# One-hot bias rows as tiles, other units behind a half-way copy, and value blocks read out after the next split: one change to a hybrid decoder layer on one core

## The chip, the core and the metric

The kernel runs on one core of a Trainium2 chip. A core has several engines that run side by side and wait for each other by semaphores: TensorE (PE in the profile; PEld is its loading of stationary operands), VectorE (DVE), ScalarE (ACT), GpSimd (POOL) and SyncE (SP, which issues most of the DMA loads). Matrix products are accumulated in PSUM and read out from there by DVE or ACT.

The metric is the device time of one execution in microseconds (us). Three runs of the kernel before took 1171.28, 1173.89 and 1175.08 us; their median, 1173.89 us, is the time before. A further execution was taken with the profiler.

## What is computed

One layer of a decoder on 256 tokens with 2048 channels, in float32. The input is normalised and multiplied by one wide matrix, the result is cut into the inputs of four mixers, and a sigmoid gate with a bias of its own weighs each mixer's output before one last product:

```python
h = rms_norm(x, g_pre[l])
proj = h @ w_in[l]
...
y_a = pool_mixer(a_val, a_gate, w_pool[l], pool_scale[l])
y_b = swa_mixer(sq, sk, sv, s_gate)
y_c = gla_mixer(cq, ck, cv, c_lr, c_gate, w_alpha[l], b_alpha[l], g_gla[l])
y_m = mem_attn(mq, m_gate, mem, g_mem[l], w_mem_kv[l])
gates = jax.nn.sigmoid(g_logits.reshape(B, S, N_BRANCH, D_MODEL) + b_merge[l])
merged = (gates[:, :, 0] * (y_a @ w_br_pool[l]) + gates[:, :, 1] * (y_b @ w_br_swa[l])
          + gates[:, :, 2] * (y_c @ w_br_gla[l]) + gates[:, :, 3] * (y_m @ w_br_mem[l]))
x = x + rms_norm(merged @ w_out[l], g_post[l])
```

The change touches the gates (`g_logits` and `b_merge`, 8192 columns of `w_in`) and the two value products `cv` (gated linear attention) and `sv` (sliding-window attention).

## The kernel before

**Products in three parts.** Every weight is loaded as float32 and split: ACT writes the rounded part `hi`, DVE the rest `lo = raw - hi` (`split_w`, L149 to L154; five buffers for each of the two). A product is then three matmuls, hi by hi, lo by hi and hi by lo (`mm3`, L156 to L160). The loads land in `raw` tiles (`load_raw`, L144, issued by SP), and a split of 1024 columns serves six or more matmuls.

**Units.** The main line of work is a list of units in program order. `b_unit` (L197) makes 128 output channels for all tokens from two half units of 16 matmuls each, eight with 512 moving columns (L208) and eight with 256 (L209); `a_block` (L162) makes up to 512 output channels for two halves of the tokens, in two PSUM buffers of the tag `acc`, which has two buffers in all. The order is: the units cq and ck, three `cv` blocks, cg, the units of the memory attention (mq, mg), those of the pooling mixer (av, ag), three `sv` blocks, those of the sliding window (sq, sk, sg). After that come the products of the four branches and the last product.

**Reading out a block.** `a_block` returns a function `finish` that reads its two accumulators out (for `cv` and `sv` two ACT copies, L550 and L831). With the argument `late`, a block calls the function of the block before it right behind its own first split (`behind()` orders those instructions after the two of the split); before the change only the blocks of the last product use that, while the `cv` and `sv` blocks call `finish` at once.

**Gates as a second stream.** The gates are computed between the units. `gates(work)` (L109) is called after each half unit and each part of a block: it adds 1.13 times the work to a credit and then takes steps from a generator while the credit is above zero; each step yields what is taken off. A half unit counts 2.8. There are eight pairs of gate blocks, `gate_pair(b, jj)` (L463), whose name in the profile is made of b and jj. A pair has three stretches:

- eight small steps `gu` (loop over u and hf, L472 to L481): one split and six matmuls each into the PSUM buffer `p1`, which starts with the bias matmul. After the fourth step ACT copies `p1` to the tile `p1c` (L480), and the next four steps go on adding into `p1`. PE may not write `p1` before that copy is done. The steps are named gu{pair}{u}{hf}: gu..11 is the fourth, gu..20 the fifth.
- eight big steps `gt` (L487 to L501): one load, three additions on DVE, two splits and twelve matmuls into four PSUM buffers q4 to q7; q5 starts with the pair's second bias matmul.
- four small steps `gv` into q5 (L510 to L518), and the gate values (tanh on ACT, L459) go out to DRAM (L461, issued by ACT).

**Bias rows.** `brow` holds the biases as 16 rows of 512 in two parts (48 rows with the gap between them), `sel` has one column for each gate block or pair with ones where its rows are. The bias matmul (L454) takes one column of `sel`, repeated 128 times by its access pattern, as the stationary operand.

**Buffers.** Temporaries of up to 2 KB per partition share the tag `c2` with seven buffers (L54): among them `p1c`, the gate values on their way out, and the temporaries of the units' read-outs.

**What sets the order.** Each engine runs its instructions in a fixed order, worked out when the kernel is built: instructions that are ready go in program order, and one further down may go first where those ahead of it aren't ready. So the order on an engine is near the program's order but not the same; for instance the bias matmul of q5 runs before the steps of `p1` in the first pair (84.36 us in the trace, the first step of p1 later).

Of the kernel before, what the change touches and what calls it, by code (L numbers as in the profile page):

```python
# [8 lines left out]
F32 = mybir.dt.float32  # L9
R = mybir.dt.float32r  # L10
# [4 lines left out]
P = 128  # L15
# [22 lines left out]
def kernel(ctx, tc, ins, out):  # L38
    nc = tc.nc
    ten, vec, act, pool, sync = nc.tensor, nc.vector, nc.scalar, nc.gpsimd, nc.sync  # L40
# [13 lines left out]
    def c2(name, shape, dt=F32):  # L54
        return big.tile(shape, dt, tag="c2", bufs=NB_C2, name=name)
# [106 lines left out]
    def a_block(name, units, stat, nw, evac, load=None, per_split=None, other=False, late=None):  # L162

        accs = [seven(f"{name}a{t}") if other else acc(f"{name}a{t}", [P, 512]) for t in range(2)]
        nk = 4 * len(units)
        for u, src in enumerate(units):
            raw = load_raw(src, 4 * nw) if load is None else load(u, src)
            nk_s = max(1, 1024 // nw) if per_split is None else per_split(u)
            for hf in range(4 // nk_s):
                hi, lo = split_w(raw[:, hf * nk_s * nw : (hf + 1) * nk_s * nw], nk_s * nw, f"{name}{u}{hf}")  # L170
                if late is not None:
                    with behind():
                        late()
                    late = None
                for t in range(2):
                    ts = slice(t * P, (t + 1) * P)
                    for kk in range(nk_s):
                        k = 4 * u + nk_s * hf + kk
                        ws = slice(kk * nw, (kk + 1) * nw)
                        sh, sl = stat(k)  # L180
                        mm3(accs[t][:, :nw], sh[:, ts], sl[:, ts], hi[:, ws], lo[:, ws], k == 0, k == nk - 1)
                if hf % 2 == 0:
                    pull(1)
                gates(nk_s * 6 * (nw / 2.4 + 14) * 1e-3)
            pull(1)

        def finish():
            for t in range(2):
                evac(t, accs[t][:, :nw])

        return finish
# [5 lines left out]
    def b_unit(name, src, mov, evac, ready=None):  # L197

        a = acc(f"{name}a", [P, 512])
        if ready is None:  # L200
            raw = load_raw(src, 2048)
        for hf in range(2):
            hi, lo = ready[hf] if ready else split_w(raw[:, hf * 1024 : (hf + 1) * 1024], 1024, f"{name}{hf}")
            for kk in range(8):
                k = 8 * hf + kk
                ws = slice(kk * P, (kk + 1) * P)
                mh, _ = mov(k)
                ten.matmul(a[:], lhsT=hi[:, ws], rhs=mov.both(k), start=(k == 0), stop=False)  # L208
                ten.matmul(a[:, :T], lhsT=lo[:, ws], rhs=mh, start=False, stop=(k == KT - 1))  # L209
            if hf == 0:  # L210
                pull(1)
                gates(2.8)
        if pinned[0]:
            with behind():
                evac(name, a)
        else:
            evac(name, a)
        pull(1)
        gates(2.8)
# [90 lines left out]
    h_at = hilo_tiles("x")  # L310
# [117 lines left out]
    brow = cst.tile([48, 512], R, name="brow")  # L428
    sel = cst.tile([48, 24], R, name="sel")
# [21 lines left out]
        yield  # L451

    def bias(o, r):
        ten.matmul(o, lhsT=sel[:, r : r + 1].to_broadcast([48, P]), rhs=brow[:], start=True, stop=False)  # L454

    gate_dram = {}

# [5 lines left out]
    def gate_pair(b, jj):  # L463


        j0, j1, n = 2 * jj, 2 * jj + 1, f"{b}{jj}"
        w = ins["w_g"]
        p1 = seven(f"p1{n}")
        bias(p1[:], 4 * b + j0)
        p1c = c2(f"p1c{n}", [P, 512])  # L470
        for u in range(4):
            raw = load_raw(w[b, j0, u], 2048)  # L472
            for hf in range(2):
                hi, lo = split_w(raw[:, hf * 1024 : (hf + 1) * 1024], 1024, f"gu{n}{u}{hf}")
                for i in range(2):
                    k = 4 * u + 2 * hf + i
                    ws = slice(i * 512, (i + 1) * 512)
                    mm3(p1[:], *tok(0, k), hi[:, ws], lo[:, ws], False, k % 8 == 7, k >= 8)
                if u == 1 and hf == 1:
                    act.activation(p1c[:], p1[:], AF.Copy)  # L480
                yield 0.8  # L481
        c11 = c2(f"c11{n}", [P, 512])
        put_gate(b, j0, 0, p1[:], c11[:])
        q4, q5, q6, q7 = [seven(f"q{i}{n}") for i in (4, 5, 6, 7)]
        bias(q5[:], 16 + 2 * b + jj)
        for kk in range(8):
            raw = new_raw()  # L487
            r4 = raw[:].rearrange("p (j u c) -> p j u c", j=2, u=2)
            u, cs = kk // 4, slice((kk % 4) * 512, (kk % 4 + 1) * 512)
            sync.dma_start(r4, w[b, j0 : j0 + 2, u : u + 3 : 2, :, cs].rearrange("j u p c -> p j u c"))  # L490
            vec.tensor_tensor(r4[:, :, 0, :], r4[:, :, 0, :], r4[:, 1, :, :], op=ALU.add)  # L491
            vec.tensor_tensor(r4[:, 1, 1, :], r4[:, 1, 1, :], r4[:, 0, 0, :], op=ALU.add)  # L492
            hi, lo = split_w(raw[:, 1024:2048], 1024, f"gt{n}{kk}a")
            st, sp = kk == 0, kk == 7
            mm3(q7[:], *quart(2, kk), hi[:, 0:512], lo[:, 0:512], st, sp)
            mm3(q6[:], *quart(1, kk), hi[:, 512:1024], lo[:, 512:1024], st, sp)
            vec.tensor_tensor(r4[:, 0, 1, :], r4[:, 0, 1, :], r4[:, 1, 1, :], op=ALU.add)  # L497
            hi, lo = split_w(raw[:, 0:1024], 1024, f"gt{n}{kk}b")
            mm3(q5[:], *quart(0, kk), hi[:, 0:512], lo[:, 0:512], False, sp)
            mm3(q4[:], *tok(1, kk + 8), hi[:, 512:1024], lo[:, 512:1024], st, sp)  # L500
            yield 6.6  # L501
        v3, c21 = c2(f"v3{n}", [P, 512]), c2(f"c21{n}", [P, 512])
        vec.tensor_tensor(p1c[:], q6[:], p1c[:], op=ALU.subtract)
        vec.tensor_tensor(v3[:], q7[:], p1c[:], op=ALU.add)
        vec.tensor_tensor(c21[:], q4[:], v3[:], op=ALU.subtract)  # L505
        put_gate(b, j0, 1, c21[:], c21[:])
        vec.tensor_tensor(v3[:], q5[:], v3[:], op=ALU.add)
        put_gate(b, j1, 1, v3[:], v3[:])
        vec.tensor_tensor(q5[:], q5[:], p1c[:], op=ALU.add)
        for u in range(2, 4):  # L510
            raw = load_raw(w[b, j1, u], 2048)
            for hf in range(2):
                hi, lo = split_w(raw[:, hf * 1024 : (hf + 1) * 1024], 1024, f"gv{n}{u}{hf}")
                for i in range(2):
                    kk = 4 * (u - 2) + 2 * hf + i
                    ws = slice(i * 512, (i + 1) * 512)
                    mm3(q5[:], *quart(3, kk), hi[:, ws], lo[:, ws], False, kk == 7, True)
                yield 0.8  # L518
        c12 = c2(f"c12{n}", [P, 512])
        put_gate(b, j1, 0, q5[:], c12[:])  # L520
# [20 lines left out]
    cv = e8("cv", [P, 2, 1024])  # L541
# [4 lines left out]
    def cv_evac(j):  # L546
        def evac(t, a):
            c0, n = CV_BLOCKS[j]
            nv = min(n, 1024 - c0)
            act.activation(cv[:, t, c0 : c0 + nv], a[:, :nv], AF.Copy)  # L550
            if nv < n:
                act.activation(lr[:, t, :], a[:, nv:n], AF.Copy)

        return evac
# [136 lines left out]
    for n in range(8):  # L691
        if n == 6:
            drain("quarters")
            pinned[0] = False
            gate_stream[0] = all_gates()
        if n < 6:
            ahead[cqk[n + 1][0]] = b_split(*cqk[n + 1])
        evac = plain_evac(gq[:, n, :], SCALE) if n < 4 else plain_evac(gk[:, n - 4, :])
        b_unit(*cqk[n], h_at, evac, ahead.pop(cqk[n][0], None))
    for j in range(3):  # L700
        c0, n = CV_BLOCKS[j]
        a_block(f"cv{j}", [ins[f"w_cv{j}"][u] for u in range(4)], h_at, n, cv_evac(j))()
    queue.append(("mnorm", m_norm()))
    queue.append(("gla", gla()))
    for h in range(4):
# [109 lines left out]
    for g in (3, 2, 1, 0):  # L815
        u = c4(f"u{g}", [P, 2, PAD + T])
# [10 lines left out]
    sv = [c4(f"sv{g}", [P, 2, 512]) for g in range(3)]  # L827

    def sv_evac(j):
        def evac(t, a):  # L830
            act.activation(sv[j][:, t, :], a, AF.Copy)  # L831

        return evac

    for j in range(3):
        a_block(f"sv{j}", [ins["w_sv"][j, u] for u in range(4)], h_at, 512, sv_evac(j))()
    yb_dram = [spill("ybd", [P, 2, 4, T], R)]
    sgate = c4("sgate", [P, 4, T])

# [141 lines left out]
    late = None  # L981
# [114 lines left out]
```

## Time and profile before

| | us |
|---|---|
| median of three runs | 1173.89 |
| least and most of them | 1171.28, 1175.08 |
| the profiled execution | 1172.68 |
| its span, first to last instruction | 1170.6 |

In the profile, a row of the timeline gives the start from the beginning of the span, the length (both in us), the engine, the line of the kernel, the operation, what it writes and reads, the shapes, and in brackets how long the engine stood idle before it and what ended the wait. A row `PE p L158 <- ACT p1c L480: 2.4, 4, 0.9` in the view of waits says that PE waited with a matmul of line 158 into p for the instruction of line 480 on ACT: 2.4 us in all, four times, 0.9 the longest. The granted TensorE clock of the core is 0.998 over the span. A matmul's length covers its whole way through the array, and the next one starts well before it ends; so the distance from start to start is what a matmul costs.

### The profile page before, as it was taken

To read this page: it belongs to the slowest core of one execution; us is meant where nothing else is said; L and a number is where in the kernel's file an instruction comes from. 1 tells how busy PE (TensorE), PEld (TensorE's weight loads), DVE (VectorE), ACT (ScalarE), POOL (GpSimd) and SP (SyncE) were. 2 spreads that over 40 slices of the span, in tenths; PEclk is the share of its full clock that TensorE was granted. 3 is DMA by queue.
4 is the path that set the end of the run, shared out by engine and by line. 5 is a ranking of instruction groups with operands and counts; after the bars stand their busy time and mean duration, and the time that the engine had idled before them with its cause. 6 is when DMAs were issued, how large, how long until landed. Compare 5 with 4: busy or idle time off the path is not lost.

```text
span 1170.6 us, 15411 instructions
## 1 busy us (share of the span) xinstructions
PE 1149.8 (98%) x5854; PEld 968.2 (83%) x5854; DVE 961.2 (82%) x1201; ACT 647.0 (55%) x823; POOL 59.0 (5%) x109
## 2 busy tenths in 40 slices
PE   9999999999999999999999999999999999999997
PEld 7887898878888888878888887888788888888887
DVE  7979798999898799889989988987898676777454
ACT  7656456665655555665566556566555543434441
POOL 0010000000101001000000000000000102110000
PEclk9999999999999999999999999999999999999999
DMA  9755679757868688777788777876778988759321
GB/s 356 316 182 193 217 251 343 277 203 281 304 238 284 217 297 289 259 251 263 276 295 315 251 263 271 294 253 231 272 252 303 372 308 306 252 206 381 118 73 73
DMA packets 79946, 303.94 MB, mean 260 GB/s; under 512 B 6224, under 2 KB 8656, under 8 KB 57344
## 3 DMA queue, kind: packets, MB, share of 16 engines
q1 hardware_dynamic: 65568, 268.45, 63.5%
q0 software_dynamic: 8976, 24.91, 6.1%
q10 hardware_dynamic: 5328, 9.60, 2.2%
q8 instruction: 46, 0.75, 0.3%
q14 instruction: 28, 0.23, 0.1%
HBM read 285.11 MB, written 17.83 MB: 259 GB/s over the span
## 4 chain that ended last, share of the span: by engine, by line
PE 76%; DVE 5%; DMA 3%; ACT 2%; issue 2%; DVEq 0%; POOLq 0%; POOL 0%; ACTq 0%
PE q L158 5%; PE q L159 5%; PE q L160 5%; DMA raw<-in_w_g 2%; PE p L158 2%; PE p L159 1%; PE p L160 1%; PE sv2a L159 1%; PE sv0a L158 1%; PE sv0a L160 1%; PE o0a L160 1%; PE sv2a L158 1%; PE o0a L158 1%; PE sv1a L158 1%; PE sv0a L159 1%
## 5 line engine op out<-in xcount | busy, mean ns | idle before, releaser
L491 DVE TENSOR_TENSOR raw<-raw 128x1024 f32<-128x1024 f32 x64 | 78.1, 1220 | 8.9 <-DMA raw<-in_w_g 8.9
L497 DVE TENSOR_TENSOR raw<-raw 128x512 f32<-128x512 f32 x64 | 44.5, 696 | 1.1
L492 DVE TENSOR_TENSOR raw<-raw 128x512 f32<-128x512 f32 x64 | 44.5, 697 | 0.5
L918 POOL DMA_DIRECT2D g<-gd x32 | 17.4, 554 | 98.6 <-DVE merged L926 66.7
L926 DVE TENSOR_TENSOR merged<-merged,g 128x512 f32<-128x512 f32 x24 | 15.5, 686 | 0.0
L710 POOL DMA_DIRECT2D cgd<-cgate x4 | 2.2, 552 | 201.7 <-DVE cgate L241 201.7
L885 POOL DMA_DIRECT2D ybd<-ybt x4 | 2.7, 678 | 174.1 <-DVE ybt L247 174.1
L853 PE MATMUL sp<-k,q 128*128 128x128 f32 (+1 forms) x48 | 10.2, 335 | 1.0 <-DVE k L226 1.0
L861 ACT ACTIVATE s<-s,st 128x384 f32<-128x384 f32 (+1 forms) x8 | 6.2, 769 | 6.7 <-DVE st L860 6.7
L853 PEld LDWEIGHTS sp<-k,q 128*128 128x128 f32 x48 | 7.4, 190 | 2.9 <-DVE k L226 1.4
L856 DVE SCALAR_TENSOR_TENSOR s<-big_cst,sp 128x128 f32<-128x128 f32 (+1 forms) x24 | 7.1, 349 | 2.0 <-PE sp L853 2.0
L246 ACT ACTIVATE xhl<-xn 128x1024 fp32r<-128x1024 f32 x4 | 4.2, 1060 | 7.0 <-DVE xn L330 7.0
L459 ACT ACTIVATE c<-c 128x512 f32<-128x512 f32 x8 | 5.0, 628 | 5.5 <-DVE c L505 3.9
L939 ACT ACTIVATE mTh<-mtp 128x512 fp32r<-128x512 f32 x8 | 4.3, 595 | 6.3 <-PE mtp L937 6.3
L459 ACT ACTIVATE c<-p 128x512 f32<-128x512 f32 x8 | 4.7, 587 | 5.1 <-PE p L160 5.1
L664 POOL TENSOR_TENSOR ms<-ms,half 128x2 f32<-128x2 f32 x4 | 5.7, 1428 | 35.2 <-DVE ms L663 35.2
L879 PE MATMUL po<-pt,sv 128*128 128x256 f32 x24 | 7.2, 384 | 0.2 <-ACT pt L874 0.2
L812 POOL DMA_DIRECT2D yad<-yat x4 | 2.7, 686 | 88.5 <-DVE yat L247 88.5
L360 DVE SCALAR_TENSOR_TENSOR mhl<-mr,vecs,mhl 128x256 fp32r<-128x256 f32 x16 | 6.8, 479 | 0.4 <-issue 0.3
L652 POOL TENSOR_TENSOR sq<-sq 128x256 f32<-128x256 f32 x4 | 4.4, 1106 | 53.0 <-ACT sq L651 53.0
L359 ACT ACTIVATE mhl<-mr,vecs 128x256 fp32r<-128x256 f32 x16 | 6.9, 495 | 0.2 <-DMA mr<-in_memT 0.2
L1003 POOL TENSOR_TENSOR opart<-opart,half 128x1 f32<-128x1 f32 x2 | 1.1, 562 | 116.0 <-DVE opart L1002 116.0
(4603 smaller groups left out, 4582.7 us busy)
## 6 DMA issues: line engine op xcount, KB each, us to landing
raw<-in_w_g SPq DMA_DIRECT2D x112, 1024.0 KB, 5.8
raw<-in_w_sqk SPq DMA_DIRECT2D x24, 1024.0 KB, 6.6
raw<-in_w_sv SPq DMA_DIRECT2D x12, 1024.0 KB, 6.5
raw<-in_w_out SPq DMA_DIRECT2D x12, 1024.0 KB, 9.6
raw<-in_w_cqk SPq DMA_DIRECT2D x8, 1024.0 KB, 15.0
raw<-in_w_cg SPq DMA_DIRECT2D x8, 1024.0 KB, 6.6
raw<-in_w_av SPq DMA_DIRECT2D x8, 1024.0 KB, 5.0
raw<-in_w_ag SPq DMA_DIRECT2D x8, 1024.0 KB, 6.0
```

The source lines that it names most:

```text
L158: ten.matmul(o, lhsT=sh, rhs=wh, start=start, stop=False, skip_group_check=again)
L159: ten.matmul(o, lhsT=sh, rhs=wl, start=False, stop=False, skip_group_check=again)
L160: ten.matmul(o, lhsT=sl, rhs=wh, start=False, stop=stop, skip_group_check=again)
L459: act.activation(dst, src, AF.Tanh, scale=0.5)
L491: vec.tensor_tensor(r4[:, :, 0, :], r4[:, :, 0, :], r4[:, 1, :, :], op=ALU.add)
L492: vec.tensor_tensor(r4[:, 1, 1, :], r4[:, 1, 1, :], r4[:, 0, 0, :], op=ALU.add)
L497: vec.tensor_tensor(r4[:, 0, 1, :], r4[:, 0, 1, :], r4[:, 1, 1, :], op=ALU.add)
L853: ten.matmul(parts[g], lhsT=q3[:, g, it * P : (it + 1) * P], rhs=k3[:, g, :nj], start=True, stop=True)
L856: vec.scalar_tensor_tensor(s[:, g, :], dist[:, g, :], SLOPES[g * 4 + hh], parts[g], op0=ALU.mult, op1=ALU.add)
L879: ten.matmul(po[:], lhsT=sv[g][:, 0, vs], rhs=pt[g][:, 0:T], start=(g == 0), stop=False)
L918: pool.dma_start(gs[t][:], gate_dram[b, j, t][:])
L926: vec.tensor_tensor(m, m, gs[t][:], op=ALU.add)
```

## The change

Three edits in one diff:

1. `bias` writes the one-hot column out as a tile `pick` of 48 by 128 from the `c2` buffers, by a DVE copy, and the matmul takes that tile as its stationary operand. There are sixteen such bias matmuls.
2. In a pair's first stretch, the step after which `p1` is copied yields 4.0, and the other seven yield 0.35 (before: 0.8 each). So the credit falls below zero after the copy, and units follow before the fifth step.
3. The `cv` and the `sv` blocks hand their `finish` to the next block as `late`; the third calls it at once.

```diff
     def bias(o, r):
-        ten.matmul(o, lhsT=sel[:, r : r + 1].to_broadcast([48, P]), rhs=brow[:], start=True, stop=False)
+        pick = c2(f"pick{r}", [48, P], R)
+        vec.tensor_copy(pick[:], sel[:, r : r + 1].bitcast(F32).to_broadcast([48, P]))
+        ten.matmul(o, lhsT=pick[:], rhs=brow[:], start=True, stop=False)
...
                 if u == 1 and hf == 1:
                     act.activation(p1c[:], p1[:], AF.Copy)
-                yield 0.8
+                    yield 4.0
+                else:
+                    yield 0.35
...
+    late = None
     for j in range(3):
         c0, n = CV_BLOCKS[j]
-        a_block(f"cv{j}", [ins[f"w_cv{j}"][u] for u in range(4)], h_at, n, cv_evac(j))()
+        late = a_block(f"cv{j}", [ins[f"w_cv{j}"][u] for u in range(4)], h_at, n, cv_evac(j), late=late)
+    late()
...
+    late = None
     for j in range(3):
-        a_block(f"sv{j}", [ins["w_sv"][j, u] for u in range(4)], h_at, 512, sv_evac(j))()
+        late = a_block(f"sv{j}", [ins["w_sv"][j, u] for u in range(4)], h_at, 512, sv_evac(j), late=late)
+    late()
```

## The prediction

> **What bounds the kernel now.** I read the page first (busy times and the 40 slices), then the waits of PE, then the instructions in order of time around each place that the diff touches.
>
> ```profile
> span 1170.6 us, 15411 instructions
> ...
> PE 1149.8 (98%) x5854; PEld 968.2 (83%) x5854; DVE 961.2 (82%) x1201; ACT 647.0 (55%) x823; POOL 59.0 (5%) x109
> ```
>
> TensorE is busy from end to end, and DVE comes second with 82%. No part of the change removes a matmul, so it can only win the short stretches in which PE stands, and it loses what it puts on PE or on a DVE that becomes late. PE's own list of waits says how much there is to win:
>
> ```profile
> PE p L158 <- ACT p1c L480: 2.4, 4, 0.9
> PE cv1a L158 <- ACT cv100h L152: 1.2, 1, 1.2
> ```
>
> Columns: microseconds in all, times, longest. The first row is the half-way copy of a pair's first product (four of eight pairs), the second is one block boundary of the gla values. No row of that list names a product of sv: those boundaries cost PE nothing today. Because a matmul counts as busy until its modelled end, I measure every loss below from start to start.
>
> **Part 1, the bias rows.** A bias is one matmul with 48 rows, whose stationary operand is one column of `sel` read 128 times. If the repeated read were what costs, the tile would save it. The trace holds 64-row matmuls with an ordinary stationary operand to compare with:
>
> ```profile
> 190.23 0.32 PE L159 MATMUL cv2a<-cv231l,xhl 128*128 128x346 f32 x1
> 190.39 0.32 PE L160 MATMUL cv2a<-cv231h,xhl 128*128 128x346 f32 x1
> 190.64 0.49 PE L454 MATMUL p<-brow,sel 48*128 48x512 f32 x1
> 191.07 0.50 PE L158 MATMUL p<-gu1000h,xhl 128*128 128x512 f32 x1
> ...
> 281.78 0.28 PE L209 MATMUL mq0a<-xhl,mq01l 128*128 128x256 f32 x1
> 281.99 0.48 PE L628 MATMUL pv<-cv,kt 64*128 64x256 f32 x1
> ...
> 282.31 0.38 PE L628 MATMUL pv<-cv,kt 64*128 64x256 f32 x1
> ...
> 282.53 0.59 PE L630 MATMUL pv<-cv,kt 64*128 64x256 f32 x2
> ...
> 283.05 0.49 PE L208 MATMUL mg0a<-xhl,mg00h 128*128 128x512 f32 x1
> ...
> 101.11 0.39 PE L159 MATMUL p<-gu0011l,xhl 128*128 128x512 f32 x1
> 101.33 0.39 PE L160 MATMUL p<-gu0011h,xhl 128*128 128x512 f32 x1
> ```
>
> In the flow a matmul of 512 columns takes 0.22 to 0.23 (101.11 to 101.33), one of 346 takes 0.16 (190.23 to 190.39), so one of 256 about 0.11. The way into the bias is 0.25 instead of 0.16, and the way out 0.43 instead of 0.23: 0.09 + 0.20 = 0.29 us lost. The 64-row group, with nothing repeated, loses the same: 0.21 instead of 0.11 on the way in; and on the way out its last matmul starts at 282.53 + 0.59 - 0.38 = 282.74, so 0.31 instead of 0.11. The loss belongs to the change in the number of rows, and the new tile has 48 rows as well. PE gains nothing here: 0, with 16 x 0.29 = 4.6 us as the far end if the repeated read were to blame after all.
>
> What it adds is 16 copies on DVE (two in each of eight pairs). The nearest row has one source in SBUF and 128 columns (durations in ns: least, median, most):
>
> ```profile
> L670 DVE TENSOR_SCALAR dg<-ident,ms x8: 279/284/364, 316.9 to 460.6; 128x128 f32<-128x128 f32 x8
> ```
>
> So 16 x 0.28 = 4.5 us of DVE. Behind a copy in DVE's queue stand the splits (`lo`) that PE takes next. How much slack DVE has there, in the stretches round the starts of pairs:
>
> ```profile
> 200.00:290.00 90.00, 88.47 (x459) 72.77 (x458) 86.39 (x108) 57.21 (x72) 2.21 (x4) 1.00 0.71 255
> 390.00:425.00 35.00, 33.95 (x169) 27.88 (x168) 28.75 (x34) 21.50 (x29) 2.19 (x4) 1.00 0.75 259
> 500.00:530.00 30.00, 29.07 (x136) 23.50 (x134) 24.96 (x30) 19.08 (x27) 0.67 (x1) 1.00 0.74 257
> ...
> 700.00:735.00 35.00, 33.40 (x159) 26.80 (x158) 28.61 (x31) 22.06 (x27) 0.70 (x1) 1.00 0.76 259
> 805.00:840.00 35.00, 34.03 (x159) 26.52 (x158) 29.07 (x35) 21.88 (x27) 0.00 (x0) 1.00 0.70 244
> ```
>
> (After the length: PE, PEld, DVE, ACT, POOL; PE's clock stands at 1.00.) Where pairs start, DVE is busy 82 to 83% (28.75 of 35, 29.07 of 35), so a 0.28 us copy is covered by its idle sixth; only in 200 to 290 (86.39 of 90) is there none left, and there at most two copies fall. I take 0.3 us on the path, between 0 and 4.5. [...]
>
> A second effect: a bias can start today as soon as its PSUM buffer is free, and PE takes both biases of a pair side by side where that suits, paying 0.29 once. With a copy ahead they may part, 0.29 each time. I take 0.4 (between 0 and 8 x 0.29 = 2.3).
>
> **Part 2, the half-way copy.** After the fourth of eight steps ACT copies `p1` out while PE may not add to it. By the credit sum (each call adds 1.13 times its work, steps are taken while the credit is above zero) the old 0.8 lets four steps out per half unit of 2.8; the new 4.0 always ends the burst at the copy, because credit never exceeds 3.2. The sum of one pair's steps stays: 8 x 0.8 = 6.4 against 7 x 0.35 + 4.0 = 6.45. The starts round the copy today:
>
> ```profile
> 101.33 0.39 PE L160 MATMUL p<-gu0011h,xhl 128*128 128x512 f32 x1
> 102.41 0.50 PE L158 MATMUL p<-gu0020h,xhl 128*128 128x512 f32 x1 [0.69 <-ACT p1c L480]
> ...
> 410.49 0.28 PE L209 MATMUL av20a<-xhl,av200l 128*128 128x256 f32 x1
> 411.12 0.50 PE L158 MATMUL p<-gu3020h,xhl 128*128 128x512 f32 x1 [0.35 <-ACT p1c L480]
> ...
> 516.87 0.47 PE L209 MATMUL ag00a<-xhl,ag000l 128*128 128x256 f32 x1
> 517.61 0.60 ACT L480 ACTIVATE p1c<-p 128x512 f32<-128x512 f32 x1 [1.33 <-DMA gd<-c]
> 518.26 0.50 PE L158 MATMUL p<-gu0120h,xhl 128*128 128x512 f32 x1 [0.93 <-ACT p1c L480]
> ...
> 822.32 0.39 PE L208 MATMUL sq21a<-xhl,sq210h 128*128 128x512 f32 x1
> 823.17 0.50 PE L158 MATMUL p<-gu3120h,xhl 128*128 128x512 f32 x1 [0.46 <-ACT p1c L480]
> ```
>
> Lost beyond the flow: 1.08 - 0.23 = 0.85; 0.63 - 0.11 = 0.52; 1.39 - 0.11 = 1.28; 0.85 - 0.23 = 0.62. I worked the credit through all calls for both versions. In the first pair the old sum already lets half a unit out between the two steps, and the new one takes the very same steps: that 0.85 stays. In the other three the two steps were neighbours and now one or two half units (16 matmuls, 8 x (0.23 + 0.11) = 2.7 us each) lie between, more than the longest wait. At stake: 0.52 + 1.28 + 0.62 = 2.4 us. I take 2.1, since the first pair shows that a half unit in between doesn't always reach PE in between. Each step's loads (SP) and splits (ACT, DVE) move with it, and the unit's own loads pass them; DMA is 0.70 to 0.76 busy in those stretches. What is late next is the second burst: four steps and a big one in a row, where before one to four ran ahead of the big one.
>
> **Part 3, the value blocks.** The one boundary that costs:
>
> ```profile
> 139.66 0.46 ACT L550 ACTIVATE cv<-cv0a 128x348 f32<-128x348 f32 x1 [5.11 <-PE cv0a L160]
> ...
> 140.25 0.32 PE L160 MATMUL cv0a<-cv031h,xhl 128*128 128x348 f32 x1
> ...
> 140.60 0.46 ACT L550 ACTIVATE cv<-cv0a 128x348 f32<-128x348 f32 x1 [0.48 <-PE cv0a L160]
> 140.96 0.77 ACT L152 ACTIVATE cv100h<-raw 128x692 fp32r<-128x692 f32 x1
> ...
> 141.78 0.59 PE L158 MATMUL cv1a<-cv100h,xhl 128*128 128x346 f32 x2 [1.22 <-ACT cv100h L152]
> 142.56 0.87 DVE L153 TENSOR_TENSOR cv101l<-raw,cv101h 128x692 fp32r<-128x692 f32 x1
> 142.70 0.19 PEld L159 LDWEIGHTS cv1a<-cv100l,xhl 128*128 128x128 f32 x1 [0.62 <-DVE cv100l L153]
> ```
>
> ACT stands 5.11 us in front of the read-out with the next split queued behind it. PE loses 1.53 - 0.16 = 1.37 and then 0.92 - 2 x 0.16 = 0.60: 1.97. With the split first, the first token half is read out by 140.12 and the second by 141.06, while PE needs them at 140.41 and six matmuls (0.95) later, 141.36: no stall. What is late next is the following split: its `hi` behind the second read-out ends near 141.8 and its `lo` 0.87 later, while PE comes for it at 140.41 + 12 x 0.16 + 0.16 = 142.5; I keep 0.3 for that. Gain 1.7 (1.4 to 2.0). The other boundaries are in that order already (cv200h at 163.00 stands ahead of the read-out of cv1), and add nothing:
>
> ```profile
> 163.00 0.77 ACT L152 ACTIVATE cv200h<-raw 128x692 fp32r<-128x692 f32 x1
> 163.68 0.44 ACT L550 ACTIVATE cv<-cv1a 128x346 f32<-128x346 f32 x1
> ```
>
> **Sum.** -1.7 - 2.1 + 0.3 + 0.4 = -3.1 us. The profiled execution took 1172.68, so 1169.6 on its scale; the median of the runs, 1173.89, lies 1.2 above it: **1170.8**. Beside the sum, the order on every engine after about 190 us (the second pair), where the steps first differ, is worked out anew when the kernel is built. In the five stretches above PE lost 1.53 + 1.05 + 0.93 + 1.60 + 0.97 = 6.1 us, 2.4 of it in part 2; the other 3.7 may go or double. I give that 2.5 either way.
>
> **Rivals.**
> *The order gives the copy's wait back* (as in the first pair): part 2 yields nothing, the block boundary holds: -1.7 + 0.7 = -1.0, 1172.9. For it: 102.41 above; against: its half unit had been split ahead, which the later units are not.
> *Slower, by buffers of 2 KB.* The tiles `pick` share seven buffers (`c2`) with `p1c`, the gate tiles on their way out and the units' temporaries. Those do run out: ACT's copy at 517.61 stood 1.33 for a gate tile's write, and DVE stood too:
>
> ```profile
> DVE pl L776 <- DMA ymd<-ymt: 2.2, 1, 2.2
> ```
>
> If at half of the sixteen picks DVE stands 1.3 with the splits queued behind, that is +10.4 - 3.8 = +6.6, 1180.5; it turns the sign for good from six such waits (7.3 us). Against: a pick lives only until its matmul, and three such waits of 3.8 us in all in the whole trace show few. [...]
> *The repeated read does cost*: another -4.6, 1166.2. The 64-row rows speak against it.
>
> **How the numbers follow.** My forecast 0.50, the order giving it back 0.26, buffers 0.14, repeated read 0.06, other 0.04. A difference of 0.3% (3.5 us), about what a measurement of this kernel tells from none, lies just beyond the forecast's -3.1: of its 0.50 some 0.26 fall below 1170.4. With the repeated read and a lucky draw in the second case faster has 0.36, slower 0.14, the same 0.50. The range reaches from the repeated read's time, 1166, to halfway into the buffers' case, 1177.
>
> **What would show it.** The rows of L454 lose 0.29 as before; the wait of cv1a on cv100h is gone; of p on p1c one of four is left; DVE has 16 more instructions and some 4.5 us more. I am wrong if picks wait for a DMA, or if new PE waits of over 2.5 us in all stand between 190 and 920 us.

## The result, and the profile after

The changed kernel takes 1184.28 us (median of four runs, 1181.95 to 1184.64) against 1172.59 for the kernel before in the same comparison: ratio 1.0097, 95% interval 1.0067 to 1.0126. It is 11.7 us slower, where -3.1 us had been forecast, and lies above the range. The profiled execution has a span of 1182.7 us, 12.1 more than before.

The page and PE's list of waits of the changed kernel (us in all, times, longest):

```profile
span 1182.7 us, 15440 instructions
...
PE 1152.4 (97%) x5854; PEld 971.4 (82%) x5854; DVE 965.6 (82%) x1217; ACT 651.0 (55%) x823; POOL 57.4 (5%) x109
```

```profile
PE q L158 <- DVE q L513: 3.3, 1, 3.3
PE p L456 <- DVE pick L455: 3.3, 3, 1.2
PE pq L665 <- ACT sqh L246: 1.9, 1, 1.9
...
PE mg1a L209 <- DVE mg10l L153: 1.1, 1, 1.1
...
PE mo L749 <- ACT mpt L745: 1.1, 1, 1.1
...
PE p L158 <- ACT p1c L482: 0.9, 2, 0.7
```

The sixteen copies cost DVE next to nothing (965.6 busy against 961.2). The waits that the change was aimed at are nearly gone (the last row; the block boundary of cv1a is no longer in the list). New ones stand at the top, and only the second names a pick. Both signs that the prediction had named for being wrong are there: one pick stands 0.4 us for a DMA, and the new waits of PE add up to far more than 2.5 us.

Where the time goes is seen by comparing when PE starts the last matmul of the same unit in two traces. The numbers are worked out from the traces (us from the span's start). The name in brackets is the pair whose start lies behind PE by then; the fourth column belongs to a run told of below, `p23`, the changed kernel without the pick tiles:

| last matmul of | before | changed | without the tiles |
|---|---|---|---|
| ck3 (pair 00 behind it) | 117.0 | 117.1 | 116.5 |
| cv1 | 163.9 | 161.2 | 160.5 |
| mq0 (pair 10 behind it) | 281.8 | 278.4 | 277.6 |
| mg1 (pair 20 behind it) | 322.9 | 323.4 | 318.8 |
| ag21 (pair 30) | 451.0 | 453.2 | 447.0 |
| ag00 (pair 01) | 531.7 | 539.4 | 527.0 |
| sg0 (pair 21) | 734.7 | 745.8 | 728.9 |
| sk21 (pair 31) | 847.4 | 858.9 | 839.3 |
| the last product | 1162.1 | 1173.9 | 1154.3 |

The block boundary wins its 2.9 us by the end of cv1. Then the changed kernel loses round the starts of the pairs, and almost nothing elsewhere: about 4 us at 20, 2 at 30, 5 at 01, 3 to 4 at 21. After the gates end, the distance stays at 11.8 to the end. Against the kernel without the tiles pair 31 loses too: 2.7 us, from 16.9 to 19.6.

What happens at such a start, pair 01, as DVE and PE see it in the changed kernel:

```profile
503.02 1.22 DVE L153 TENSOR_TENSOR gu0100l<-raw,gu0100h 128x1024 fp32r<-128x1024 f32 x1 [0.39 <-ACT gu0100h L152]
...
507.20 1.06 ACT L152 ACTIVATE gu0101h<-raw 128x1024 fp32r<-128x1024 f32 x1 [1.69 <-PE q L160]
...
508.30 1.22 DVE L153 TENSOR_TENSOR gu0101l<-raw,gu0101h 128x1024 fp32r<-128x1024 f32 x1 [2.04 <-ACT gu0101h L152]
...
509.66 1.22 DVE L153 TENSOR_TENSOR gu0110l<-raw,gu0110h 128x1024 fp32r<-128x1024 f32 x1
...
510.86 0.39 PE L160 MATMUL q<-gv3031h,quarter 128*128 128x512 f32 x1
511.02 1.23 DVE L153 TENSOR_TENSOR gu0111l<-raw,gu0111h 128x1024 fp32r<-128x1024 f32 x1
...
512.16 0.21 DVE L455 CAST pick<-sel 48x128 fp32r<-48x128 f32 x1
512.43 0.49 PE L456 MATMUL p<-brow,pick 48*128 48x512 f32 x1 [1.18 <-DVE pick L455]
512.85 0.50 PE L158 MATMUL p<-gu0100h,xhl 128*128 128x512 f32 x1
```

and in the kernel before:

```profile
500.27 0.50 PE L454 MATMUL p<-brow,sel 48*128 48x512 f32 x1
500.61 0.40 PE L454 MATMUL q<-brow,sel 48*128 48x512 f32 x1
500.91 1.22 DVE L153 TENSOR_TENSOR gu0100l<-raw,gu0100h 128x1024 fp32r<-128x1024 f32 x1 [0.39 <-ACT gu0100h L152]
500.93 0.50 PE L158 MATMUL p<-gu0100h,xhl 128*128 128x512 f32 x1
```

Before, the bias stands ahead of the first split, and the first product begins in the moment in which that split does. In the changed kernel `pick` (512.16) stands in DVE's order behind four splits (503.02 to 511.02) that serve the very products which wait for it. The first split waits 9.8 us for its use (503.02 to 512.85), and by then four of the five split buffers hold splits of the new pair. Already at 507.20 ACT's next split had to wait until PE had used up one of the pair before, and whatever the other units need next queues behind.

PE also loses work that it could have done meanwhile. Ahead of pair 21 the kernel without the tiles runs that pair's first products while DVE finishes pair 11 (`q` of L511 there, L513 in the changed kernel), and its first `gv` product comes without a wait:

```profile
699.84 0.58 PE L158 MATMUL p<-gu2100h,xhl 128*128 128x512 f32 x1
...
701.46 0.50 PE L159 MATMUL p<-gu2100l,xhl 128*128 128x512 f32 x1 [0.61 <-DVE gu2100l L153]
...
702.73 0.44 PE L158 MATMUL q<-gv1120h,quarter 128*128 128x512 f32 x1
```

In the changed kernel those products wait for the bias, and PE stands 3.3 us in front of the same `gv` product (714.11, in the last section). So most of the new waits in the list name something else than `pick`.

### The profile page after: what moved, and what is told of

Read it like the earlier page. It is cut to its first block, busy times and chain, and to the rows that moved or that the text cites. A ratio compares the mean times of both kernels' runs of the same rounds, so it can differ in the third digit from the quotient of the medians.

```text
span 1182.7 us, 15440 instructions
## 1 busy us (share of the span) xinstructions
PE 1152.4 (97%) x5854; PEld 971.4 (82%) x5854; DVE 965.6 (82%) x1217; ACT 651.0 (55%) x823; POOL 57.4 (5%) x109
## 4 chain that ended last, share of the span: by engine, by line
PE 85%; DVE 5%; DMA 4%; issue 2%; ACT 2%; SPq 0%; DVEq 0%; POOLq 0%; POOL 0%; ACTq 0%
PE q L158 6%; PE q L160 6%; PE q L159 6%; DMA raw<-in_w_g 2%; PE p L158 2%; DMA raw<-in_w_km 2%; PE p L160 1%; PE p L159 1%; PE kma L387 1%; PE sv0a L158 1%; PE sv0a L160 1%; PE sv0a L159 1%; PE o0a L158 1%; PE o0a L160 1%; PE o1a L159 1%
## 5 line engine op out<-in xcount | busy, mean ns | idle before, releaser
L882 ACT ACTIVATE pt<-tp 128x384 f32<-128x384 f32 x12 | 5.7, 481 | 3.1 <-PE tp L880 3.1
L456 PE MATMUL p<-brow,pick 48*128 48x512 f32 x8 | 4.0, 494 | 3.3 <-DVE pick L455 3.3
```

## The experiments

Each run is put against the kernel before on the same chip at the same time (1172.49, 1172.65 and 1171.6 us in the three comparisons); the differences to it are what the tables compare. Where an edit is shown, `...` marks lines left out.

### Each part alone

The first four runs take one part alone, or leave the tiles out.

`p1_only`: the first hunk of the diff.

```diff
+        pick = c2(f"pick{r}", [48, P], R)
+        vec.tensor_copy(pick[:], sel[:, r : r + 1].bitcast(F32).to_broadcast([48, P]))
+        ten.matmul(o, lhsT=pick[:], rhs=brow[:], start=True, stop=False)
```

> The kernel before with the pick tiles alone. Theory A (the tiles: a copy on DVE and a buffer of the seven stand in front of a pair's first matmul, which PE then waits for): slower by 6 to 14 us, and the waits of L454's successor on the copy appear as in the changed kernel (3.3 us and more). Theory B (the new yields: a denser second burst): within 2 us of before. Theory C (nothing by itself, only the order that falls out anew): anywhere within 4 us.

Measured: 1189.59, ratio 1.0144 (1.0128 to 1.0160), +17.1 us.

`p2_only`: the second hunk.

```diff
-                yield 0.8
+                    yield 4.0
+                else:
+                    yield 0.35
```

> The kernel before with the new yields alone (4.0 after the half-way copy, 0.35 else). Theory A: faster by 1 to 3 us, the waits of p on p1c fall from four to one. Theory B: slower by 6 to 14 us, with PE waiting around the starts of the pairs 01 and 21 as in the changed kernel (5.5 and 3.9 us). Theory C: anywhere within 4 us.

Measured: 1168.33, ratio 0.9967 (0.9956 to 0.9979), -4.2 us. Of the waits of p on p1c one is left:

```profile
PE p L158 <- ACT p1c L480: 0.7, 1, 0.7
```

`p3_only`: the third and fourth hunks.

```diff
-        a_block(f"cv{j}", [ins[f"w_cv{j}"][u] for u in range(4)], h_at, n, cv_evac(j))()
+        late = a_block(f"cv{j}", [ins[f"w_cv{j}"][u] for u in range(4)], h_at, n, cv_evac(j), late=late)
+    late()
...
```

> The kernel before with the late read-out of the cv and sv blocks alone. All theories: faster by 1.5 to 3 us, all of it between the end of cv0 and the end of cv1, none at the sv blocks (the changed kernel gained 2.9 us between those two ends).

Measured: 1170.79, ratio 0.9989 (0.9980 to 0.9998), -1.7 us. In its trace the last matmul of cv1 comes 3.1 us earlier than before, 2.9 of it gained since the end of cv0, and at the sv blocks the distance doesn't change. Its span is 3.0 us shorter (1167.6 against 1170.6), while the medians of the timed runs differ by 1.7.

`p23`: the changed kernel without the first hunk.

> The changed kernel without the pick tiles (bias from the repeated column as before). Theory A: faster than before by 3 to 5 us. Theory B: slower by 3 to 12 us. Theory C: within 4 us of before.

Measured: 1165.55, ratio 0.9941 (0.9928 to 0.9953), -6.9 us. So parts 2 and 3 together win what they win alone and 1 us more, and the tiles cost 11.7 + 6.9 = 18.6 us on top of that, 17.1 alone. Theory A stands in kind, B and C are out; but the tiles alone cost more than the 6 to 14 us that A had named, and the other parts won more than the 1 to 3 and the 3 to 5. Still open was what of the tiles costs: the shared buffers or DVE's queue.

### Buffer or queue

Four corners: the copy by DVE or by GpSimd, into the shared buffers or into one of its own. DVE with shared buffers is the changed kernel itself, and the edits of this part are made to it.

```diff
-        pick = c2(f"pick{r}", [48, P], R)
+        pick = big.tile([48, P], R, tag="pick", bufs=1, name=f"pick{r}")
...
-    ones_r = cst.tile([P, P], R, name="ones_r")
-    vec.tensor_copy(ones_r[:], ones[:])
+    ones_r = cst.tile([P, 2], R, name="ones_r")
+    vec.tensor_copy(ones_r[:], ones[:, 0:2])
```

> The changed kernel with one buffer of its own for pick, outside the seven shared ones (ones_r, of which two columns are read, is made two columns wide to make room). Theory A1 (the shared buffers: the copy has to wait for one, stands behind three or four splits in DVE's order, and these hold the split buffers): back to the time without the tiles, 1164 to 1168 us, and the bias stands ahead of its pair's first split again. Theory A2 (DVE's queue: any copy there in front of a pair's first matmul comes late): still 1178 to 1186 us.

```diff
-        vec.tensor_copy(pick[:], sel[:, r : r + 1].bitcast(F32).to_broadcast([48, P]))
+        pool.tensor_copy(pick[:], sel[:, r : r + 1].bitcast(F32).to_broadcast([48, P]))
```

> The changed kernel with the copy on GpSimd, still into the seven shared buffers. Theory A1: as slow as the changed kernel, 1178 to 1188 us, the bias behind two to four splits. Theory A2: 1164 to 1170 us, since GpSimd is idle at those places.

The fourth corner has both edits:

> The changed kernel with the copy on GpSimd and into a buffer of its own: the fourth corner beside the changed kernel (DVE, shared), pick_own (DVE, own) and pick_pool (GpSimd, shared). If what pick_own still loses against the kernel without the tiles (6 us) comes from DVE's queue, 1164 to 1168 us; if it comes from the bias matmul having to wait for any copy at all (the first pair above all, where PE stood 0.6 and 1.3 us and then ran at half clock), 1169 to 1174 us.

And the copies alone, into a buffer of their own (with the same edit to `ones_r`), with the old matmul behind them:

```diff
+        pick = big.tile([48, P], R, tag="pick", bufs=1, name=f"pick{r}")
+        vec.tensor_copy(pick[:], sel[:, r : r + 1].bitcast(F32).to_broadcast([48, P]))
         ten.matmul(o, lhsT=sel[:, r : r + 1].to_broadcast([48, P]), rhs=brow[:], start=True, stop=False)
```

> The changed kernel with the sixteen DVE copies into a buffer of their own, which no matmul reads (the bias matmul takes the repeated column as before). This is the price of 16 x 0.21 us of DVE alone. Both theories: within 2 us of the kernel without the tiles (1163.5 to 1168 us); if DVE's load itself were the cost, 1175 us and more.

| against before, us (ratio, interval) | shared buffers | a buffer of its own |
|---|---|---|
| copy by DVE | +11.7 (1.0097, 1.0067 to 1.0126) | -1.0 (0.9989, 0.9979 to 0.9999) |
| copy by GpSimd | +11.0 (1.0090, 1.0074 to 1.0105) | -5.8 (0.9950, 0.9938 to 0.9962) |
| copies that no matmul reads | | -7.0 (0.9946, 0.9933 to 0.9958) |

Without the tiles it is -6.9. With a buffer of its own and the copy on GpSimd the tile costs 1.1 us; with DVE 5.9; in the shared buffers 18 to 19, whichever engine copies (though a part of pick_pool's is GpSimd's own: its copies take 0.28 to 7.2 us there, and PE waits 4.8 us for two of them). The buffer is what counts most; `pick_own` lies in neither of the spans named for it (1164 to 1168 and 1178 to 1186), since DVE's queue has a share of its own. `copy_unread` says little about DVE's load in place: with nothing waiting for them all sixteen copies went ahead at once, between 74.8 and 80.2 us:

```profile
L455 DVE CAST pick<-sel x16: 209/220/222, 74.8 to 80.2; 48x128 fp32r<-48x128 f32 x16
```

That it is the place in the order shows when the pairs are counted out (worked out from the traces, pairs 00, 10, 20, 30, 01, 11, 21, 31). First, how many of a pair's own DVE splits have started before its bias; then the time from the first of these splits to the first product in `p1` (us):

| | splits ahead of the bias | first split to first product |
|---|---|---|
| without the tiles | 0 4 4 0 0 3 0 0 | 3.1 5.2 6.5 -1.1 0.0 4.2 -0.4 -0.3 |
| changed kernel | 2 4 4 3 4 3 3 4 | 6.4 5.3 10.8 7.1 9.8 4.7 11.7 7.2 |
| pick_pool | 1 3 4 3 4 3 3 4 | 5.4 5.3 12.1 7.8 8.6 4.7 10.5 5.9 |
| pick_own | 0 3 4 0 0 3 0 0 | 2.7 5.2 6.5 -1.0 -1.2 4.2 -0.5 -0.3 |

A buffer of its own puts the first bias of every pair back to where it was (in pair 10 behind three splits in place of four); GpSimd alone doesn't. The pairs that lose time against the kernel without the tiles (20, 30, 01, 21, 31) are those whose first product is late here by 4 to 12 us.

In the changed kernel the wait for a buffer hardly shows on DVE: it stood only 0.4 us in front of a pick. On GpSimd, which has little else to do (57.4 us busy in the whole span of the changed kernel), the wait shows. In `pick_pool` the copy for pair 20 starts when a gate value has been written out to DRAM, and that for pair 01 when DVE has read the `p1c` of pair 30 for the last time; the gate values and `p1c` are tiles of the seven shared buffers. Four of the sixteen copies wait for such a write:

```profile
284.21 0.46 POOL L455 CAST pick<-sel 48x128 fp32r<-48x128 f32 x1 [10.83 <-DMA gd<-v]
...
297.34 0.79 PE L456 MATMUL p<-brow,pick 48*128 48x512 f32 x1
...
507.33 0.28 POOL L455 CAST pick<-sel 48x128 fp32r<-48x128 f32 x1 [9.02 <-DVE q L513]
...
512.98 0.49 PE L456 MATMUL p<-brow,pick 48*128 48x512 f32 x1
```

The same rows show that the wait itself is not the whole cost. The copies are done at 284.67 and 507.61, and PE comes to the bias 12.7 and 5.4 us later; in every pair it comes at least 2.9 us after the copy's end. So what costs is the late place of the bias in the order that is worked out when the kernel is built. That the shared buffers give it that place follows from the own buffer curing it; how the order is worked out no row shows. Six in place of seven shared buffers would have been the counter-test; no run has that.

Where pick_own still loses is its first pair, where both bias matmuls have been pulled forward and the second copy hasn't been:

```profile
83.72 0.50 PE L456 MATMUL p<-brow,pick 48*128 48x512 f32 x1
84.53 0.49 PE L456 MATMUL q<-brow,pick 48*128 48x512 f32 x1 [0.31 <-DVE pick L455]
84.95 0.50 PE L208 MATMUL ck1a<-xhl,ck10h 128*128 128x512 f32 x1
86.47 0.38 PE L209 MATMUL ck1a<-xhl,ck10l 128*128 128x256 f32 x1 [1.01 <-DVE ck10l L153]
...
87.52 0.63 PE L208 MATMUL ck1a<-xhl,ck10h 128*128 128x512 f32 x1
87.95 0.41 PE L209 MATMUL ck1a<-xhl,ck10l 128*128 128x256 f32 x1
```

PE waits for the second pick, then for the split queued behind the picks, and then runs 0.43 from start to start in place of 0.23 for some microseconds: 3.4 us lost to copy_unread by the end of ck1, more than half of the 5.9. DVE itself stood there for the one buffer, which the bias before had to give back:

```profile
84.25 0.22 DVE L455 CAST pick<-sel 48x128 fp32r<-48x128 f32 x1 [4.29 <-PE p L456]
85.06 0.22 DVE L455 CAST pick<-sel 48x128 fp32r<-48x128 f32 x1 [0.59 <-PE q L456]
85.20 1.21 DVE L153 TENSOR_TENSOR ck10l<-raw,ck10h 128x1024 fp32r<-128x1024 f32 x1
```

The rest is spread over smaller shifts, some 2 us of it round pair 01, and stays unexplained. own_pool lands inside the first span that was named for it, so of the two causes DVE's queue is the one: a copy on GpSimd is waited for too (1.2 us in all, three times 0.4, again for the one buffer), but nothing else is queued behind it. Two buffers of its own on DVE might win back part of the 5.9; no run has that.

### The number of rows

The prediction held that a bias loses 0.29 us because it has 48 rows between matmuls of 128, not because a column is read repeatedly. `k128` is p23 with both operands filled up with zeros:

```diff
-    brow = cst.tile([48, 512], R, name="brow")
-    sel = cst.tile([48, 24], R, name="sel")
+    brow = cst.tile([P, 512], R, name="brow")
+    sel = cst.tile([P, 24], R, name="sel")
...
-        raw = c2("braw", [48, 512])
+        raw = c2("braw", [P, 512])
...
-        one = c2("bsel", [48, 24])
-        vec.tensor_tensor(one[:, 0:16], ident[0:48, 0:16], ident[0:48, 32:48], op=ALU.add)
+        one = c2("bsel", [P, 24])
+        pool.memset(one[:], 0.0)
+        vec.tensor_tensor(one[0:48, 0:16], ident[0:48, 0:16], ident[0:48, 32:48], op=ALU.add)
...
-        ten.matmul(o, lhsT=sel[:, r : r + 1].to_broadcast([48, P]), rhs=brow[:], start=True, stop=False)
+        ten.matmul(o, lhsT=sel[:, r : r + 1].to_broadcast([P, P]), rhs=brow[:], start=True, stop=False)
```

> The changed kernel without the tiles, and brow and sel made 128 rows tall with zeros below row 48, so that a bias matmul has as many rows as its neighbours; the column is still read 128 times. If the number of rows causes the 0.29 us that a bias loses, the rows of the bias flow like the others (0.23 from start to start) and it is faster by up to 16 x 0.29 = 4.6 us, 1161 to 1164 us; if the repeated read causes it, nothing changes, 1164.5 to 1167 us.

Measured: 1161.8, ratio 0.9910 (0.9897 to 0.9924), -10.9 us, 3.9 better than p23. That is not much more than a new order alone can move (next part), so the rows decide: the bias flows like its neighbours, 0.16 in and 0.23 out, with the column still read 128 times:

```profile
186.56 0.32 PE L159 MATMUL cv2a<-cv231l,xhl 128*128 128x346 f32 x1
186.72 0.32 PE L160 MATMUL cv2a<-cv231h,xhl 128*128 128x346 f32 x1
186.88 0.39 PE L455 MATMUL p<-brow,sel 128*128 128x512 f32 x1
187.11 0.40 PE L158 MATMUL p<-gu1000h,xhl 128*128 128x512 f32 x1
```

### How much a new order is worth

The prediction gave the newly drawn order 2.5 us either way. Two runs of k128 move the gates' share by 0.01:

```diff
-GATE_SHARE = 1.13
+GATE_SHARE = 1.12
```

> k128 with the gates' share at 1.12 in place of 1.13: nothing is added or taken away, only the points at which the gate steps fall between the units move, so this is the size of a new drawing of the order. Within 3 us of k128's 1161.8 either way.

Measured: 1159.12, ratio 0.9892 (0.9879 to 0.9904), -12.5 us.

> k128 with the gates' share at 1.14: the same question from the other side. Within 3 us of k128's 1161.8 either way.

Measured (1.14 in place of 1.12): 1163.82, ratio 0.9947 (0.9929 to 0.9965), -7.8 us.

Against k128's -10.9 that is 1.6 better and 3.1 worse: a difference of 2 to 3 us between two versions can be nothing but the order. It also bounds what is said above about a microsecond or two: that own_pool is 1.1 us slower than p23, and that parts 2 and 3 win 1 us more together, may be the order. share_112 is the fastest kernel of this study and beats both the kernel before and the changed one, by 1.1% and about 2%.

## Why the prediction was wrong

**The step that failed** is the cost of the copy in part 1: "I take 0.3 us on the path, between 0 and 4.5". It measured the copy's length and DVE's idle share, and the copy is indeed cheap: 0.21 us each (0.28 had been taken from the nearest row). But the cost isn't in the copy. The old bias needed nothing but a PSUM buffer, and in five of the eight pairs of the kernel without the tiles it stands ahead of all its pair's splits; the new one needs one of seven shared buffers as well, and in every pair of the changed kernel it stands behind two to four splits. The runs put that at 18.6 us (changed kernel against p23), 12.7 of it gone with a buffer of its own and 5.9 more without the copy. About 3 of the 18.6 are the clock that fell behind two of the stalls (last section). The upper end of 4.5 us was wrong as a bound, since it bounded the time of the copy and not what waits for it.

**The rival that came true in part** is the one by buffers, to which 0.14 was given, with +6.6 us. Its cause, the shared buffers, is what the runs show; its mechanism was not quite that. It let DVE stand in front of a pick until a buffer came free. DVE hardly stands there (0.4 us): the order made at build time has the splits go first, and it is PE that waits, and with it the split buffers. The argument against it, "a pick lives only until its matmul, and three such waits of 3.8 us in all in the whole trace show few", looked for the shortage among waits of the finished order, where most of it no longer shows. What stands in line behind the new tile should have been written down: pick, bias, first product, and the five split buffers behind that.

**Part 1, rest.** PE gains nothing from the tile: right. In the changed kernel all sixteen biases stand alone, where three pairs had stood side by side; 0.4 had been allowed for that, three pairs at 0.29 are 0.9. That the 0.29 belongs to the number of rows is shown by the rows of k128; of 16 x 0.29 = 4.6 us, 3.9 came back.

**Part 2** was right in its mechanism and too small: -2.1 taken, -4.2 measured. The first pair keeps its wait exactly as the credit sum had it (101.58 to 102.65 in the changed kernel, 1.07, against 1.08):

```profile
101.58 0.39 PE L160 MATMUL p<-gu0011h,xhl 128*128 128x512 f32 x1
102.65 0.50 PE L158 MATMUL p<-gu0020h,xhl 128*128 128x512 f32 x1 [0.69 <-ACT p1c L482]
```

What was missed stands in the trace of before under another name. At pair 21 PE also stood round the half-way copy, but the first matmul behind it was one of the attention's, which waited for DVE's `k`, so the list of waits files it under that:

```profile
719.51 0.39 PE L208 MATMUL sg0a<-xhl,sg00h 128*128 128x512 f32 x1
719.71 0.60 ACT L480 ACTIVATE p1c<-p 128x512 f32<-128x512 f32 x1 [0.32 <-PE p L160]
...
720.89 0.49 PE L853 MATMUL sp<-k,q 128*128 128x128 f32 x2 [0.99 <-DVE k L226]
```

1.38 instead of 0.23: 1.15 us more to win, and in p2_only it is gone, as half a unit stands there instead. How much of it was the copy's is not shown: the copy ends at 720.31, `k` at 720.83, and `k` ended the wait. A further 1.1 us of waits in pair 31's first big step (832.8 to 834.8 in the trace of before) went too; that wasn't foreseen and may be the order.

**Part 3** was right in the place: the gain lies at the one boundary named, and at the others there is none. Its size was taken too small: -1.7 (1.4 to 2.0), and the trace has 2.9 there. That the medians give just -1.7 is in part luck, since their interval reaches from -2.3 to -0.2.

**The newly drawn order**, 2.5 us either way, is of the size that the two runs with another share show.

So without part 1 the sum would have been -3.8, and the kernel without it won 6.9.

## What to carry to other kernels

An instruction that can start on nothing but its own output buffer is worth keeping so: a small tile from a crowded pool in front of a chain can cost the chain its place in line, which was far more than the tile's length here (18.6 us for sixteen copies of 0.21 us each). Price such a tile by what cannot start before it and what that holds meanwhile, and put it in a buffer of its own (12.7 us here) and on an engine with nothing queued behind (4.8 more), or do without it. Where the bias matmul of 48 rows stood between matmuls of 128, zeros up to 128 rows gave back a quarter of a microsecond each time (3.9 us over the sixteen).

## What the runs showed that was not expected

**PE's clock fell after some stalls.** At the end of pair 11 in the changed kernel PE stood 3.3 us for DVE, and the matmuls after it came 0.43 apart in place of 0.23 for about 3 us, 1.6 us in all:

```profile
714.11 0.80 PE L158 MATMUL q<-gv1120h,quarter 128*128 128x512 f32 x1 [3.29 <-DVE q L513]
714.70 0.63 PE L159 MATMUL q<-gv1120l,quarter 128*128 128x512 f32 x1
715.13 0.63 PE L160 MATMUL q<-gv1120h,quarter 128*128 128x512 f32 x1
...
717.25 0.40 PE L159 MATMUL q<-gv1121l,quarter 128*128 128x512 f32 x1
717.48 0.40 PE L160 MATMUL q<-gv1121h,quarter 128*128 128x512 f32 x1
```

The granted clock over 713 to 718 us is 0.66 in that trace. In pick_own shorter waits stand ahead of such a stretch: behind 0.3 and 1.0 us of waiting and slow starts between 83.7 and 86.5 the clock over 85 to 91 us is 0.72. The changed kernel has a second one, behind waits of 0.7 and 0.2 us (at 531.59 and 532.18) at the first big step of pair 01: the clock is 0.50 from 532.9 to 536.3. Not every wait of that length has such a stretch behind it: behind the 1.2 us for cv100h in the kernel before the clock over the next microseconds is 1.00 (143 to 148), and behind the 1.9 us for sqh in the changed kernel (396.41) the matmuls come 0.23 apart, at a clock of 1.00 over 395 to 400. So the length of the one wait doesn't tell here whether the clock falls, and what does no row shows. Each of the two stretches of the changed kernel costs about 1.6 us, so the stall of 3.3 us came to about 4.9.

```profile
85.00:91.00 6.00, 4.99 (x19) 4.02 (x19) 5.59 (x9) 2.51 (x4) 0.00 (x0) 0.72 0.42 131
```

```profile
713.00:718.00 5.00, 3.89 (x11) 3.10 (x12) 1.05 (x2) 1.55 (x2) 0.00 (x0) 0.66 1.02 353
```

```profile
532.90:536.30 3.40, 3.40 (x9) 2.68 (x8) 2.88 (x4) 2.03 (x2) 0.00 (x0) 0.50 1.03 336
```

(The first row is of pick_own, the others of the changed kernel; after the length PE, PEld, DVE, ACT, POOL, then the clock.)
